# Fixed orders in the pooling stage and the convolution's tail, two-row biases, early row stores, joined closings and respread units

## The chip, the cores and the metric

The kernel runs on one core of a Trainium2 chip. The metric is the device time of one execution in microseconds (us). The kernel before takes 1178.71 us (median of three runs, 1175.62 to 1179.85). Its profiled execution took 1184.47 us, of which the span of the trace is 1182.6 us.

## The reference

A trunk of four layers on 256 tokens of width 1024, all in float32. Layers 0 and 3 mix tokens with latent attention, layer 1 with a Conformer convolution, layer 2 with a causal pooling mixer; each is followed by a feed-forward part of inner width 4096. Shift, scale and gate of every part come from a conditioning vector c.

```
c_act = silu(c)
for i in range(4):
    mod = c_act @ ada_w[i] + ada_b[i]                      # 6 rows of 1024
    sh_m, sc_m, gt_m, sh_f, sc_f, gt_f = split(mod, 6)
    h = rmsnorm(x, g[i,0]) * (1 + sc_m) + sh_m
    y = mla(h) | conv(h) | pool(h)                         # by layer
    x = x + gt_m * rmsnorm(y, g[i,1])
    h = rmsnorm(x, g[i,2]) * (1 + sc_f) + sh_f
    y = square(relu(h @ w1[i])) @ w2[i]
    x = x + gt_f * rmsnorm(y, g[i,3])

conv: u = (a[:, :D] * sigmoid(a[:, D:])),  a = h @ w_pw1 + b_pw1
      u = depthwise_causal_conv(u, w_dw, width 31) + b_dw
      y = silu(layernorm(u, ln_g, ln_b)) @ w_pw2 + b_pw2
pool: p_g = trailing mean of h over 2, 4, 8, 16 tokens (by channel group) - h
      y = (p_g @ w_g + b_g) * scale
```

## The kernel before, in words

Tokens stand as two blocks of 128, t = 0 and 1, the width as halves of 512 columns, n = 0 and 1. Every weight block of 128 x 1024 (a tile `raw`, five slots) is fetched by the sync engine (SP), rounded by ScalarE to a part `hi` (L173), and the rest `lo` is formed by VectorE (L174); six slots each. A product then takes three matmuls, hi with hi, lo with hi, hi with lo. SP's queue is written in program order. Of the other engines the order is chosen by a scheduler from its own estimates, except where `line` or `nosync` fixes one instruction behind another, and `tc.issue_after` holds a group behind an instruction.

The conditioning rows are made beside the rest of the work. A *unit* is 128 rows of `ada_w` for two of the six rows (a tile `araw`, 1 MB, NADA = 4 slots); eight units give one group of rows, tile `adap` in PSUM. In the feed-forward parts and the convolution VectorE adds units up into `acc`, two instructions of 128 x 1024 for each (L221, L223), and TensorE closes the sum with a product with ones (`ada_flush`, L265, `adap<-acc,ones_c`): a closing. Between the parts TensorE does a unit itself (`adap<-araw,c_act`). Then `ada_row` (L240 to L244) adds the bias; `spread` stores a row to DRAM and fetches it back for all 128 partitions, both on GpSimd's (POOL's) queue.

How many units are done where stands in two tables, MIX for the token mixers and FF for the feed-forward parts: units by step, units at the boundary ahead of the part, and how many are fetched ahead at its end (L702 to L725):

```
if c == CF:            # CF = 14
    ada_fetch(ahead)
...
rowblock([w2[i, 2 * cc + k] for k in range(2)], ...)
```

A feed-forward part has sixteen steps c. Step c makes h(c) = h @ w1 (L652, L655), r (L704, L705), relu and square (L706, L707), gh and gl (L709, L710), then the step's units; the product with w2 (`y`, L583 to L587) runs one step behind. So behind h(14) stands y(13), with the weights that SP fetches after the `ahead` units.

The convolution ends with a tail: taps of the depthwise product by blocks (L1060), transposes to tokens (`ctok`), LayerNorm (L1126 to L1132), transposes back (`sT_ps`, L1149), SiLU (L1155), and the product with w_pw2. The pooling stage takes its tokens from `boundary` (squares, scaling, residual, L500 to L570) block by block, forms the means as a product with a banded matrix (`pT_ps`, L1214 for the sixteen tokens that reach into block 1, the spill, and L1221), and multiplies with small weights (L1258) on top of a bias row (L1251).

Of the kernel before, what the change touches and what calls it, by code (L numbers as in the profile page):

```python
# [51 lines left out]
def tile_trunk(ctx: ExitStack, tc: tile.TileContext, x, cT, pos, invf, ada_w, ada_bg,  # L52
# [49 lines left out]
    ones_r = cp.tile([1, P], F32R, name="ones_r")  # L102
    V.tensor_copy(ones_r, ones_f[0:1])
# [134 lines left out]
    def ada_row(i, g, pt, put=lambda eng, ins: ins):  # L238
# [7 lines left out]
        rows[(i, g)] = row  # L246

# [67 lines left out]
    def spread(t, row, j):  # L315
        d = dr.tile([2, 512], F32, tag="row", name="rowd")
        ins = nc.gpsimd.dma_start(d, row[64 * j:64 * j + 64:32])
        if gate["pool"] is not None:
            nosync(ins, gate["pool"])
        nc.gpsimd.dma_start(t, d.rearrange("a n -> (a n)").unsqueeze(0).to_broadcast([P, D]))  # L320

    def bcast(tag, row, j):
        t = act.tile([P, D], F32, tag=f"bc_{tag}", name=f"bc_{tag}")
        spread(t, row, j)
# [5 lines left out]
    def gate_row(i):  # L330
        if (i, 1) in rows and i not in sent:
            sent.add(i)
            bcast("g", rows[(i, 1)], 0)


    def prep(row):
        bcast("a", row, 1)
        bct["sh"] = row
# [183 lines left out]
    def boundary(ys, units, planes=None, tokens=None, early=None, first=None):  # L522
# [16 lines left out]
        if not final:  # L539
            r = rsqrt_eps(*cols(ms))  # L540
            if tokens is not None:
                tokens(xa, r)
                low = early()
            else:
# [114 lines left out]

    def rowblock(srcs, lh, ll, y, first, last, tiles_first=False):  # L660
# [21 lines left out]
    def ffn(i, h, units, ahead, mid, first):  # L682
        hh, hl = h
        pair = both[0]
        bcast("g", rows[(i, 1)], 1)
# [100 lines left out]
    def mla(i, h, units, ahead):  # L786
# [3 lines left out]
        with tc.tile_pool(name=f"mla{i}", bufs=1) as mp:  # L790
# [239 lines left out]
            if (i, 2) in rows:  # L1030
                prep(rows[(i, 2)])
# [8 lines left out]
    def conv(i, h, units, ahead, first):  # L1040
        j = i // 3
        hh, hl = h
        with tc.tile_pool(name=f"conv{i}", bufs=1) as vp:
# [42 lines left out]
            for m in range(KT):  # L1086
                if m + 2 < KT:
                    for p in range(2):
                        fetch(w_pw1[j, m + 2, p])
                if m == 0:  # L1090
# [28 lines left out]
            prep(rows[(i, 2)])  # L1119
            shift_rows()  # L1120
            sh_, sl_ = planes()
            un = []
            for t in range(NT):
                st = sm.tile([P, 2, 6], F32, tag="st", name="st")
                for n in range(2):
                    V.bn_stats(st[:, n], ctok[t][n])  # L1126
                mv = sm.tile([P, 2], F32, tag="mv", name="mv")
                V.bn_aggr(mv, st)
                r = rsqrt_eps(mv[:, 1:2])
                xn = tmp.tile([P, D], F32, tag="xa", name="un")  # L1130
                for n in range(2):
                    V.tensor_scalar(xn[:, 512 * n:512 * n + 512], ctok[t][n], mv[:, 0:1], r,  # L1132
                                    ALU.subtract, ALU.mult)
                un.append(xn)
            ada(units[8])
            ada_flush()
            scope[0] = None
            y = y_banks()
            for t in range(NT):
                ts = slice(t * P, (t + 1) * P)  # L1140
                for n in range(2):
                    ns = slice(512 * n, 512 * n + 512)
                    T.matmul(y[t][n], ones_r, b2h[:, ns], start=True, stop=False, skip_group_check=True)
                    T.matmul(y[t][n], ones_r, b2l[:, ns], start=False, stop=False, skip_group_check=True)
                for g in range(2):
# [7 lines left out]
                    for k in range(4):  # L1153
# [7 lines left out]
                     [sl_[:, k] for k in range(4)], y, False, False, tiles_first=True)  # L1161
# [6 lines left out]
    def pool_consts(pp, j):  # L1168
# [5 lines left out]
        spread(shb, bct["sh"], 0)  # L1174
        return psc, band, shb

    def pool(i, head, consts, units, ahead):
# [15 lines left out]
        fetch(pool_b[j])  # L1193
        wp = [load(pool_w[j, k], gains) for k in range(2)]
        bias = fetched.pop((pool_b[j].tensor.name, pool_b[j].offset))
        V.tensor_tensor(bias, bias, psc[0:1, :], op=ALU.mult)
# [12 lines left out]
        def means(t, h, b=None):  # L1209
            if b is None:  # L1210
                b = bank("h", "pT_ps")
                for k in range(4 if t else 0):
                    kk = 4 * h + k
                    T.matmul(b[:, k * P:k * P + 16], hs[0][:, kk * P:(kk + 1) * P],  # L1214
                             band[:, kk // 2, 0, P:P + 16], start=(k == 0), stop=False,
                             skip_group_check=True)
                if t and len(hs) == 1:
                    return b
            for k in range(4):
                kk = 4 * h + k  # L1220
                T.matmul(b[:, k * P:(k + 1) * P], hs[t][:, kk * P:(kk + 1) * P],  # L1221
                         band[:, kk // 2, t, 0:P], start=(t == 0 and k == 0), stop=True,
                         skip_group_check=True)
            o = (slice(None), slice(4 * h, 4 * h + 4), slice(t * P, (t + 1) * P))
            b = b.rearrange("p (k t) -> p k t", k=4)
            gate["act"] = line("act", A.copy(ph[o], b))
# [4 lines left out]
            return low  # L1231

        ahead1 = []

        def early():
            low = [means(0, h) for h in range(2)]
            ahead1.append(means(1, 0))
            return low
# [5 lines left out]
        bcast("g", rows[(i, 1)], 0)  # L1244
        prep(rows[(i, 2)])
        ada(units)
        y = y_banks()
        for t in range(NT):
            ts = slice(t * P, (t + 1) * P)
            for n in range(2):  # L1250
                T.matmul(y[t][n], ones_f[0:1], bias[:, 512 * n:512 * n + 512], start=True,  # L1251
# [166 lines left out]
```

## Time and profile before

| | before |
|---|---|
| median of the runs (us) | 1178.71 |
| profiled execution (us) | 1184.47 |
| span of its trace (us) | 1182.6 |
| TensorE busy | 1138.4 us, 96% |
| VectorE busy | 850.6 us, 72% |
| ScalarE busy | 645.3 us, 55% |
| GpSimd busy | 54.1 us, 5% |

The attention of layer 0 ends at about 160 us; the feed-forward parts run from about 168 to 340, 488 to 662, 703 to 877 and 1002 to 1171 us, the convolution from 360 to 469 and the pooling stage from 662 to 692. Engine names in the rows: PE is TensorE, PEld its weight load, DVE VectorE, ACT ScalarE, POOL GpSimd, SPq the sync engine's DMA queue. A time in brackets is idle time ahead of an instruction, with what ended it.

### The profile page before, as it was taken

Reading aid. Unit: us, or ns where it says so; the run is one execution under the profiler, and the core shown is the slowest. Engines: PE = TensorE matmul, PEld = TensorE weight load, DVE = VectorE, ACT = ScalarE, POOL = GpSimd, SP = SyncE. Lnnn points to the kernel's source line nnn. Section 1 sums busy time; section 2 is a strip of 40 time slices with the busy share of each in tenths; the row PEclk is TensorE's granted clock in tenths of the full one; section 3 lists DMA queues with packets and bytes.
Section 4 is the critical chain, followed back from the end, with each engine's and each line's share of the span. In section 5 each row is a group of like instructions: output and inputs, shape, how many; then the busy total and the mean of one; then the engine's idle time right before and its main releaser. Section 6 shows DMA issues by size and latency. Waiting matters only on the chain. (4 is left out here: it accounts for less than half of the span.)

```text
span 1182.6 us, 17593 instructions
## 1 busy us (share of the span) xinstructions
PE 1138.4 (96%) x6706; PEld 923.5 (78%) x6706; DVE 850.6 (72%) x1197; ACT 645.3 (55%) x1145; POOL 54.1 (5%) x127
## 2 busy tenths in 40 slices
PE   7899999999999999999999999999997999999997
PEld 4667778788778867888887677878877878888886
DVE  3689787877766665787876778787876995755554
ACT  3355576556553244755564366555545675756553
POOL 1000010000010010000000110000011001000000
PEclk9999999999999988999999899999998999999999
DMA  9878759787617785778896479888644522766550
GB/s 332 304 290 311 298 208 347 270 329 290 245 53 236 256 322 213 272 272 351 315 343 256 187 278 364 311 311 323 246 134 157 170 81 80 250 199 191 183 193 35
DMA packets 73383, 290.00 MB, mean 245 GB/s; under 512 B 9986, under 2 KB 15234, under 8 KB 61012
## 3 DMA queue, kind: packets, MB, share of 16 engines
q1 hardware_dynamic: 70484, 280.44, 65.1%
q0 software_dynamic: 2816, 8.46, 2.0%
q8 instruction: 52, 0.85, 0.3%
q14 instruction: 31, 0.25, 0.1%
HBM read 286.57 MB, written 2.29 MB: 244 GB/s over the span
## 5 line engine op out<-in xcount | busy, mean ns | idle before, releaser
L174 DVE TENSOR_TENSOR lo<-raw,hi 128x1024 fp32r<-128x1024 f32 (+2 forms) x335 | 392.0, 1192 | 98.4 <-ACT hi L173 69.0
L173 ACT CAST hi<-raw 128x1024 fp32r<-128x1024 f32 (+2 forms) x335 | 335.1, 1028 | 78.6 <-PE y L587 39.4
L652 PE MATMUL h<-hT,hi 128*128 128x512 f32 x960 | 240.4, 392 | 0.0
L652 PEld LDWEIGHTS h<-hT,hi 128*128 128x128 f32 x960 | 175.8, 188 | 37.7 <-issue 3.4
L583 PE MATMUL y<-hi,gh 128*128 128x512 f32 x512 | 200.3, 393 | 1.5 <-ACT hi L173 1.5
L586 PE MATMUL y<-lo,gh 128*128 128x512 f32 x512 | 200.1, 391 | 0.2
L587 PE MATMUL y<-hi,gl 128*128 128x512 f32 x512 | 199.0, 390 | 0.0
L655 PEld LDWEIGHTS h<-hT,lo 128*128 128x128 f32 x960 | 131.0, 190 | 14.9 <-issue 5.9
L704 ACT COPY r<-h 128x256 f32<-128x256 f32 x120 | 44.5, 371 | 175.8 <-PE h L655 175.7
L655 PE MATMUL h<-hT,lo 128*128 128x256 f32 x960 | 136.0, 283 | 0.0
L223 DVE SCALAR_TENSOR_TENSOR acc<-araw,c_act,acc 128x1024 f32<-128x1024 f32 x106 | 130.7, 1279 | 0.4 <-DMA araw<-in_ada_w_dram 0.4
L583 PEld LDWEIGHTS y<-hi,gh 128*128 128x128 f32 x512 | 96.3, 188 | 22.8 <-ACT hi L173 2.4
L587 PEld LDWEIGHTS y<-hi,gl 128*128 128x128 f32 x512 | 96.1, 188 | 21.8 <-issue 0.8
L586 PEld LDWEIGHTS y<-lo,gh 128*128 128x128 f32 x512 | 96.4, 188 | 18.5 <-DVE lo L174 1.0
L705 DVE TENSOR_TENSOR r<-h,r 128x256 f32<-128x256 f32 x120 | 50.5, 421 | 39.8 <-ACT r L704 39.2
L710 DVE TENSOR_TENSOR gl<-r,gh 128x512 fp32r<-128x512 f32 x60 | 41.4, 690 | 50.2 <-ACT gh L709 50.2
L706 ACT ACTIVATE r<-r 128x512 f32<-128x512 f32 x60 | 37.9, 632 | 35.2 <-DVE r L705 35.2
L583 PE MATMUL y<-hi,hT 128*128 128x512 f32 x96 | 39.4, 412 | 0.0
L707 ACT ACTIVATE r<-r 128x512 f32<-128x512 f32 x60 | 37.9, 632 | 1.7
L586 PE MATMUL y<-lo,hT 128*128 128x512 f32 x96 | 38.8, 405 | 0.0
L587 PE MATMUL y<-hi,hT 128*128 128x512 f32 x96 | 38.6, 404 | 0.0
L709 ACT CAST gh<-r 128x512 fp32r<-128x512 f32 x60 | 37.2, 620 | 1.4
(257 smaller groups left out, 1486.8 us busy)
## 6 DMA issues: line engine op xcount, KB each, us to landing
raw<-in_w_dram SPq DMA_DIRECT2D x256, 512.0 KB, 5.8
araw<-in_ada_w_dram SPq DMA_DIRECT2D x96, 1024.0 KB, 6.4
raw<-in_w_pw_dram SPq DMA_DIRECT2D x24, 512.0 KB, 5.7
raw<-in_w_o_dram SPq DMA_DIRECT2D x16, 512.0 KB, 3.2
u<-ud SPq DMA_DIRECT2D x32, 132.0 KB, 2.8
raw<-in_w_ukv_dram SPq DMA_DIRECT2D x8, 512.0 KB
bc_g<-rowd POOLq DMA_DIRECT2D x8, 512.0 KB, 4.0
bc_a<-rowd POOLq DMA_DIRECT2D x7, 512.0 KB, 6.7
```

The source lines that it names most:

```text
L173: put(A.copy(h, raw), "act")
L174: put(V.tensor_tensor(l, raw, h.bitcast(F32), op=ALU.subtract), "dve")
L223: V.scalar_tensor_tensor(acc, raw[:, sl], ck, acc, op0=ALU.mult, op1=ALU.add)
L583: mm = T.matmul(o, ah, bh, start=start, stop=False, skip_group_check=True)
L586: T.matmul(o, ah, bl, start=False, stop=False, skip_group_check=True)
L587: return T.matmul(o, al, bh, start=False, stop=stop, skip_group_check=True)
L652: T.matmul(b, w(0, kk), pair[:, :, kk], start=(kk == 0), stop=False, skip_group_check=True)
L655: T.matmul(b[:, 0:S], w(1, kk), pair[:, 0, kk], start=False, stop=(kk == KT - 1), skip_group_check=True)
L704: A.copy(rf, hb[:, S:])
L705: V.tensor_tensor(rf, hb[:, 0:S], rf, op=ALU.add)
L706: A.activation(r, r, AF.Relu)
L710: gli = V.tensor_tensor(gl, g2, gh.bitcast(F32), op=ALU.subtract)
```

## The change

- Closings: the four matmuls of a closing or of a unit are issued in the order j = 2, 3, 0, 1, each fixed behind the one before, so that they stand in one run.
- Rows are stored to DRAM inside `ada_row` (`stage`, eight buffers); `spread` only fetches.
- Biases: `bias_rows` makes one tile with the rounded bias in row 0 and the rest in row 32; one fp32r matmul of 33 rows for each half and block replaces two single rows (convolution) or one float32 row (pooling).
- Convolution's tail: the first four w_pw2 blocks are fetched in the loop's last two turns, the shift rows made at turn m = 2, LayerNorm's instructions are in a fixed order, no unit and no closing remain in the tail behind LayerNorm (its closing stands ahead of the last taps), the bias comes after the first row block.
- Pooling stage: block 1's squares and scaling come ahead of block 0's copies, block 0's products between block 1's steps, all in fixed orders; constants are loaded at the start of the feed-forward part before.
- Tables: MIX and FF respread the units.

```
 def ada_mm(lhsT, raw, stop):
...
-        for j in range(4):
+        mm = None
+        for j in (2, 3, 0, 1):
+            prev = mm
             mm = T.matmul(grp["pt"][32 * j:32 * j + 32, :], lhsT, raw[j // 2][:, HALF[j % 2]],
                           start=first, stop=stop)
+            if prev is not None:
+                nosync(mm, prev)
...
+    def stage(i, g, j):
+        d = dr.tile([2, 512], F32, tag="row", name="rowd", bufs=8)
+        nc.gpsimd.dma_start(d, rows[(i, g)][64 * j:64 * j + 64:32])
+        staged[(i, g, j)] = d
...
 boundary:
         v1 = [y_scaled(1, ys, 0)]
+        if tokens is not None:
+            tokens(xa, r)
         y_squares(1, ys, 1, m1)
         r1 = rsqrt_eps(*cols(m1), eng=V)
         v1.append(y_scaled(1, ys, 1))
+        if tokens is not None:
+            low = early()
...
         residual(1, v1, r1)
+        if tokens is not None:
+            low[0][0]()
         ms = squares(1)
         r = rsqrt_eps(*cols(ms))
         if tokens is not None:
+            low[1][0]()
+            early()
             xa = scaled(1)
-            low[0]()
+            low[0][1]()
             tokens(xa, r)
-            low[1]()
+            low[1][1]()
...
+    def bias_rows(src, gain=None):
+        raw = raws.tile([P, D], F32, tag="raw", name="bias")[0:33]
+        G.memset(raw, 0.0)
+        for p in (0, 32):
+            nc.sync.dma_start(raw[p:p + 1], src)
+        if gain is not None:
+            V.tensor_tensor(raw, raw, gain[0:33], op=ALU.mult)
+        r = raws.tile([P, D], F32R, tag="raw", name="bias_r")[0:33]
+        A.copy(r, raw)
+        V.tensor_tensor(r[32:33], raw[32:33], r[32:33].bitcast(F32), op=ALU.subtract)
+        return r
...
 conv:
+                else:
+                    for k in range(2):
+                        fetch(w_pw2[j, 2 * (m + 2 - KT) + k])
+                if m == 2:
+                    prep(i, 2)
+                    shift_rows()
...
-            b2h, b2l = load(b_pw2[j])
             wp = [load(w_pw2[j, k]) for k in range(4)]
+            bias = bias_rows(b_pw2[j])
+            ada_flush()
...
-            ada(units[8])
-            ada_flush()
...
             rowblock(wp, [sh_[:, k] for k in range(4)],
-                     [sl_[:, k] for k in range(4)], y, False, False, tiles_first=True)
+                     [sl_[:, k] for k in range(4)], y, True, False, tiles_first=True)
+            for t in range(NT):
+                for n in range(2):
+                    T.matmul(y[t][n], ones_r, bias[:, 512 * n:512 * n + 512], start=False,
+                             stop=False, skip_group_check=True)
             ada_fetch(ahead)
...
 pool:
+        def early():
+            if not spilt:
+                parts = [means(0, h) for h in range(2)]
+                spilt.append(spill(0))
+                return parts
+            y.extend(y_banks())
+            biased(0)
+            product(0, 0)
 
         head(tokens=tokens, early=early)
-        for low in [means(1, 0, ahead1[0]), means(1, 1)]:
+        for k in range(2):
+            fetch(w1[i, 0, k])
+        ada_fetch(ahead)
+        spilt.append(spill(1))
+        parts = [means(1, h, spilt[h]) for h in range(2)]
+        for high, _ in parts:
+            high()
+        for _, low in parts:
             low()
...
+        biased(1)
+        product(0, 1)
+        product(1, 0)
+        product(1, 1)
         ada(units)
-        y = y_banks()
...
     MIX = {
         0: ([2, 4, 2, 3, 3, 2], 0, 1),
-        1: ([0, 0, 2, 0, 1, 2, 1, 0, 1], 2, 3),
-        2: (2, 4, 3),
+        1: ([0, 0, 2, 1, 1, 1, 1, 0, 0], 1, 3),
+        2: (1, 4, 2),
...
     FF = {
-        0: ([1, 1, 1, 1, 1, 2, 1, 1, 1, 1, 1, 1, 1, 1, 0, 0], 1, 3),
-        1: ([1, 1, 1, 2, 1, 1, 2, 1, 1, 2, 1, 1, 1, 1, 0, 0], 2, 4),
-        2: ([1, 1, 1, 1, 2, 1, 2, 1, 2, 1, 1, 2, 1, 2, 1, 0], 2, 0),
+        0: ([1, 2, 1, 1, 2, 1, 1, 2, 1, 1, 2, 1, 1, 2, 1, 0], 1, 3),
+        1: ([2, 1, 1, 2, 1, 1, 2, 1, 1, 1, 1, 1, 1, 1, 1, 0], 2, 4),
+        2: ([1, 1, 1, 1, 1, 1, 1, 1, 1, 1, 2, 1, 1, 2, 2, 0], 1, 0),
```

SP's queue at the end of the second feed-forward part (layer 1), before: `raw<-in_w_dram` are weights of w1 and w2, `araw` units.

```order
138 L197 DMA araw<-in_ada_w_dram 128x2048
139 L1170 DMA psc<-in_pool_s_dram 128x1024
140 L1172 DMA band<-in_pool_band_dram 128x1152
141 L155 DMA raw<-in_w_dram 128x1024 x4
142 L197 DMA araw<-in_ada_w_dram 128x2048
143 L155 DMA raw<-in_w_dram 128x1024 x4
144 L197 DMA araw<-in_ada_w_dram 128x2048 x2
145 L200 DMA bg<-in_ada_bg_dram 4x1024
146 L197 DMA araw<-in_ada_w_dram 128x2048 x2
147 L155 DMA raw<-in_w_dram 128x1024 x8
```

The same queue and place after the change.

```order
145 L200 DMA bg<-in_ada_bg_dram 4x1024
146 L155 DMA raw<-in_w_dram 128x1024 x4
147 L197 DMA araw<-in_ada_w_dram 128x2048
148 L155 DMA raw<-in_w_dram 128x1024 x4
149 L197 DMA araw<-in_ada_w_dram 128x2048 x5
150 L155 DMA raw<-in_w_dram 128x1024 x8
```

Ahead of the eight weights stand five `araw` now, the unit of c = 14 and the four fetched ahead, where there were the four; with four slots the last of the five takes the slot of the first.

VectorE at the same place, before: `r` and `gl` are the feed-forward part's, `acc` a unit, `lo` a weight.

```order
469 L710 TENSOR_TENSOR gl<-r,gh 128x512
470 L223 SCALAR_TENSOR_TENSOR acc<-araw,c_act,acc 128x1024 x2
471 L705 TENSOR_TENSOR r<-h_6137,r 128x256
472 L705 TENSOR_TENSOR r<-h_6156,r 128x256
473 L174 TENSOR_TENSOR lo<-raw,hi 128x1024 x2
474 L710 TENSOR_TENSOR gl<-r,gh 128x512
475 L174 TENSOR_TENSOR lo<-raw,hi 128x1024 x5
```

VectorE there after the change.

```order
464 L742 TENSOR_TENSOR gl<-r,gh 128x512
465 L223 SCALAR_TENSOR_TENSOR acc<-araw,c_act,acc 128x1024 x2
466 L737 TENSOR_TENSOR r<-h_6155,r 128x256
467 L737 TENSOR_TENSOR r<-h_6174,r 128x256
468 L742 TENSOR_TENSOR gl<-r,gh 128x512
469 L223 SCALAR_TENSOR_TENSOR acc<-araw,c_act,acc 128x1024 x2
470 L240 TENSOR_TENSOR row_6206<-adap,bg 128x512
471 L242 TENSOR_TENSOR row_6206<-row_6206,bg 128x512
472 L174 TENSOR_TENSOR lo<-raw,hi 128x1024 x8
```

The eight `lo` moved from both sides of gl(14) (rows 473 to 475) to behind the unit of c = 14 (row 469).

ScalarE in the pooling stage, before: `junk` are squares summed up (`y` the stage's input by halves, `xs` the tokens), `hT<-pT_ps` the means.

```order
387 L135 ACTIVATE junk,msy<-y_4861 128x512
388 L135 ACTIVATE junk,msy<-y_4862 128x512
389 L135 ACTIVATE junk,ms<-xs 128x512 x2
390 L135 ACTIVATE junk,msy<-y_4863 128x512
391 L1226 CAST hT<-pT_ps 128x4x128 x2
392 L135 ACTIVATE junk,msy<-y_4864 128x512
393 L135 ACTIVATE junk,ms<-xs 128x512 x2
394 L1226 CAST hT<-pT_ps 128x4x128 x2
```

ScalarE there after the change.

```order
379 L135 ACTIVATE junk,msy<-y_4898 128x512
380 L135 ACTIVATE junk,msy<-y_4899 128x512
381 L135 ACTIVATE junk,ms<-xs 128x512 x2
382 L135 ACTIVATE junk,msy<-y_4900 128x512
383 L135 ACTIVATE junk,msy<-y_4901 128x512
384 L1262 CAST hT<-pT_ps 128x4x128
385 L135 ACTIVATE junk,ms<-xs 128x512 x2
386 L1262 CAST hT<-pT_ps 128x4x128 x3
```

The second half's squares of block 1 (row 392 before, 383 now) moved ahead of the copies of block 0's means.

## Rows read from the trace of the kernel before

**Rows 1.** Busy time by stretch: us; PE, PEld, DVE, ACT, POOL; clock; DMA; GB/s.

```profile
436.70:450.40 13.70, 13.70 (x42) 8.69 (x35) 7.54 (x14) 7.06 (x18) 1.17 (x2) 0.50 0.86 348
...
672.20:682.50 10.30, 10.30 (x36) 7.53 (x35) 4.96 (x9) 0.96 (x3) 3.22 (x6) 0.50 0.67 277
703.00:880.00 177.00, 175.98 (x885) 144.49 (x884) 143.92 (x159) 101.62 (x148) 1.63 (x4) 1.00 0.79 293
890.70:894.10 3.40, 3.40 (x15) 2.83 (x15) 2.14 (x7) 2.59 (x9) 1.52 (x3) 0.50 0.17 46
```

**Rows 2.** TensorE's timeline, end of the second feed-forward part: start, us, instruction.

```profile
635.97 1.11 PE L655 MATMUL h<-hT,lo 128*128 128x256 f32 x8
637.01 1.07 PE L265 MATMUL adap<-acc,ones_c 128*32 128x512 f32 x8
639.60 1.19 PE L583 MATMUL y<-hi,gh 128*128 128x512 f32 x4 [1.52 <-ACT hi L173]
```

**Rows 3.** The sync engine's queue there: start, us, issues.

```profile
623.21 9.17 SPq L197 DMA_DIRECT2D araw<-in_ada_w_dram  x2
632.48 12.87 SPq L155 DMA_DIRECT2D raw<-in_w_dram  x8
```

**Rows 4.** VectorE's timeline there.

```profile
629.55 2.48 DVE L223 SCALAR_TENSOR_TENSOR acc<-araw,c_act,acc 128x1024 f32<-128x1024 f32 x2
...
639.58 1.23 DVE L174 TENSOR_TENSOR lo<-raw,hi 128x1024 fp32r<-128x1024 f32 x1 [1.63 <-ACT hi L173]
...
643.18 0.68 DVE L710 TENSOR_TENSOR gl<-r,gh 128x512 fp32r<-128x512 f32 x1
```

**Rows 5.** TensorE's timeline, one half of a split closing.

```profile
221.02 1.05 PE L265 MATMUL adap<-acc,ones_c 128*32 128x512 f32 x4
```

**Rows 6.** Tile adap, closings: what ended TensorE's wait, us, times.

```profile
  DVE acc L223: 1.7, 2
```

**Rows 7.** TensorE's timeline, units ahead of the convolution.

```profile
340.43 1.92 PE L265 MATMUL adap<-araw,c_act 128*32 128x512 f32 x16
```

**Rows 8.** TensorE's timeline, taps; the later two with a closing between.

```profile
396.46 3.69 PE L1060 MATMUL dw_ps<-u,dg 128*32 128x256 f32 x64
...
416.18 2.79 PE L1060 MATMUL dw_ps<-u,dg 128*32 128x256 f32 x42
...
420.73 1.36 PE L1060 MATMUL dw_ps<-u,dg 128*32 128x256 f32 x10
```

**Rows 9.** ScalarE's timeline, convolution's tail.

```profile
445.92 2.91 ACT L1155 ACTIVATE sv<-sT_ps,cv_lb,cv_lg 128x128 f32<-128x128 f32 x8 [4.59 <-PE sT_ps L1149]
```

**Rows 10.** TensorE's timeline, first work behind the convolution's last product.

```profile
468.87 1.92 PE L265 MATMUL adap<-araw,c_act 128*32 128x512 f32 x16
```

**Rows 11.** ScalarE's timeline, pooling stage.

```profile
663.39 0.60 ACT L135 ACTIVATE junk<-y 128x512 bf16<-128x512 f32 x1
...
668.64 0.60 ACT L135 ACTIVATE junk<-y 128x512 bf16<-128x512 f32 x1
```

**Rows 12.** VectorE's timeline, pooling stage.

```profile
673.71 1.42 DVE L1203 SCALAR_TENSOR_TENSOR xa<-xa,r,shb 128x512 f32<-128x512 f32 x2 [0.24 <-POOL r L121]
```

**Rows 13.** TensorE's timeline, pooling stage.

```profile
673.32 3.78 PE L1251 MATMUL y<-raw,ones_f 1*128 1x512 f32 x4
677.03 1.89 PE L1214 MATMUL pT_ps<-band,xa 128*128 128x16 f32 x8
...
679.55 3.35 PE L1221 MATMUL pT_ps<-band,xa 128*128 128x128 f32 x16
...
691.88 1.16 PE L395 MATMUL hT_ps<-dg,xa 128*128 128x128 f32 x8 [1.20 <-ACT dg L389]
```

**Rows 14.** ScalarE's timeline, step 14 of the second feed-forward part.

```profile
637.12 0.37 ACT L704 COPY r<-h 128x256 f32<-128x256 f32 x1 [2.42 <-PE h L655]
637.99 0.63 ACT L706 ACTIVATE r<-r 128x512 f32<-128x512 f32 x1 [0.49 <-DVE r L705]
```

**Rows 15.** TensorE's timeline, ahead of the last attention.

```profile
890.55 2.17 PE L412 MATMUL hT_ps<-ident,xa 128*128 128x128 f32 x8 [3.62 <-DVE xa L406]
```

More of the change, by code (lines that the diff above doesn't have):

```diff
@@ L246, in ada_row @@
         rows[(i, g)] = row
+        for j in ((0, 1) if g == 1 else (1,)):
+            stage(i, g, j)
+        if (i, g) == (2, 0):
+            stage(i, g, 0)
     def sum_tiles():
@@ L332, in gate_row, with prep @@
             sent.add(i)
[L333 to L338, printed above, removed]
+            bcast("g", i, 1, 0)
+    def prep(i, g):
+        bcast("a", i, g, 1)
+        bct["sh"] = rows[(i, g)]
     def shift_rows(row=None):
@@ L1140, in conv @@
                 ts = slice(t * P, (t + 1) * P)
[L1141 to L1144, printed above, removed]
                 for g in range(2):
@@ L1192, in pool @@
             fetch(pool_w[j, k])
-        fetch(pool_b[j])
         wp = [load(pool_w[j, k], gains) for k in range(2)]
-        bias = fetched.pop((pool_b[j].tensor.name, pool_b[j].offset))
-        V.tensor_tensor(bias, bias, psc[0:1, :], op=ALU.mult)
+        bias = bias_rows(pool_b[j], psc)
         hs = []
@@ L1230, in low, with product @@
                                                           op=ALU.subtract))
-            return low
-        ahead1 = []
-        def early():
-            low = [means(0, h) for h in range(2)]
-            ahead1.append(means(1, 0))
-            return low
-        head(tokens=tokens, early=early)
-        for low in [means(1, 0, ahead1[0]), means(1, 1)]:
+            return high, low
+        def product(t, low):
+            ts = slice(t * P, (t + 1) * P)
+            for g in range(4):
+                for k in range(2):
+                    ws = slice((2 * (g % 2) + k) * 256, (2 * (g % 2) + k) * 256 + 256)
+                    for q in ((0, 1), (0,))[low]:
+                        line("pe", T.matmul(y[t][g // 2][:, 256 * (g % 2):256 * (g % 2) + 256],
+                                            (ph, pl)[low][:, 2 * g + k, ts], wp[g // 2][q][:, ws],
+                                            start=False, stop=(low == 1 and k == 1),
+                                            skip_group_check=True))
@@ new lines, in biased @@
+        def biased(t):
+            for n in range(2):
+                line("pe", T.matmul(y[t][n], ones_r, bias[:, 512 * n:512 * n + 512],
+                                    start=True, stop=False, skip_group_check=True))
+        y = []
+        spilt = []
+        def early():
+            if not spilt:
[5 more added lines that the diff above has]
+            product(0, 0)
@@ L1242, in pool @@
+        head(tokens=tokens, early=early)
+        for k in range(2):
+            fetch(w1[i, 0, k])
[5 more added lines that the diff above has]
+        for _, low in parts:
             low()
         gate["free"] = 0
-        bcast("g", rows[(i, 1)], 0)
-        prep(rows[(i, 2)])
-        ada(units)
-        y = y_banks()
[L1248 to L1251, printed above, removed]
-                         stop=False, skip_group_check=True)
-            for low in range(2):
-                for g in range(4):
-                    for k in range(2):
-                        ws = slice((2 * (g % 2) + k) * 256, (2 * (g % 2) + k) * 256 + 256)
-                        for q in ((0, 1), (0,))[low]:
-                            T.matmul(y[t][g // 2][:, 256 * (g % 2):256 * (g % 2) + 256],
-                                     (ph, pl)[low][:, 2 * g + k, ts], wp[g // 2][q][:, ws],
-                                     start=False, stop=(low == 1 and k == 1),
-                                     skip_group_check=True)
```

74 lines of the change are left out of this document (36 added, 38 removed).

## The prediction

> **What bounds the kernel now.** I read the table by stage first, then TensorE's timeline at the places the diff touches, then the queues that feed it. In a feed-forward stage TensorE is the bound: in the third one it works 175.98 of 177 us at full clock, with twenty units summed on VectorE beside it [rows 1]. So a matmul taken out there is worth its duration, and a VectorE or DMA instruction is worth nothing until it makes TensorE wait. Between the stages latency decides, and two stretches run at half clock, 13.7 us in the convolution's tail and 10.3 us in the pooling stage [rows 1]; the reader is to see 0.50 in the column after POOL. The wait that matters most for this change is small now: at 639.60 the last but one row block of the second feed-forward stage waits 1.52 us for the hi of its weights [rows 2]. On the sync engine's queue, which issues in program order, the last fetch ahead is held until 632 and the eight weights only follow at 632.48 [rows 3]. It is held by its slot: VectorE's sum for c = 13 ends at 632.03 [rows 4].
>
> All durations are from the profiled execution (1184.47 us, span 1182.6); the median of the runs is 1178.71. I add the sum to the median, since it is a difference.
>
> **The change, part by part.**
>
> *Closings (TensorE).* A closing split by j is two runs of 1.05 us with other matmuls between (one of them in [rows 5]); whole it is one run of 1.07 [rows 2]: 1.03 less. The feed-forward stages hold seven split closings and one whole one, 7 x 2.10 + 1.07 = 15.8; afterwards nine whole ones (respreading makes one more), 9 x 1.07 = 9.6: -6.1. VectorE's sums held closings up twice, 1.7 us in all [rows 6]; I take -1.0 (0 to -1.7). The first layer's last closing becomes whole, -1.0. At the entry of the convolution one unit remains of two, half of 1.92 [rows 7]: -0.96. In the convolution a closing stood among the taps, in 5.91 us (416.18 to 422.09) that otherwise take 3.69 [rows 8], so 2.2; afterwards there is a split one, 2.1, and a whole one, 1.07: +0.95. Together **-8.1**, and with the waits at either end -7 to -9.
>
> *Convolution tail.* One unit on TensorE, four bias matmuls and the shift rows leave it, and the normalisation of the second token block is pinned behind the first, so its transposes come earlier. On the other side, all sixteen SiLU activations now stand ahead of hi and lo of the last weights, on ScalarE and VectorE: in the trace the last eight of them end at 448.8 [rows 9]. With the clock at full throughout I get the last y product 4.5 us before 468.87 [rows 10]; if it still drops, about nothing. I take **-3.5**, bounds -6 to +1. Memset, two small DMAs, copy and subtraction of the two-row bias lie on POOL, the sync queue, ScalarE and VectorE ahead of the first row block, beside its taps; without that cover one ScalarE pass and one VectorE pass, about 2.4 us at the length of a lo, 1.23 [rows 4], and the +1 holds part of that.
>
> *Pooling stage.* Of token block 1, the squares of the first half end at about 664.1, the second half's only start at 668.64, behind the two copies of block 0 [rows 11]. The change puts them first: 4.5 us. Block 1's band matmuls start at 679.55 although their input is ready at 673.71 + 1.42 = 675.1 [rows 12]: four bias matmuls, 3.78 us, and a spill of 1.89 at half clock stand in front [rows 13]. These biases become four fp32r matmuls and block 0's products fill the wait. So input at 675.1 - 4.5 = 670.6, 1.8 us for the spill and hand-over, start at 672.4. From there to the first transposes of the feed-forward stage it took 12.3 us (691.88); I keep 11.3, since two of the four units in between go, and half of their 1.92 us lies on the chain: 683.7 instead of 691.88, -8.2. TensorE now waits about 2.7 us ahead of 672.4, and I charge 0.8 for a lower clock behind it: **-7.4**. Least gain -2 (the shorter matmuls alone), most -9.5 (half clock gone too).
>
> *Earlier row stores.* The store goes to POOL's queue as soon as a row is known, the broadcast later: the broadcast starts sooner by one store. The trace shows no broadcast that ends a wait in the rows above; nothing, and a store at a bad place in POOL's order at most 1 us.
>
> *Units respread: what I expect to cost.* After the change the second feed-forward stage has a unit at c = 14, where there was none, and the same four fetches ahead. The fourth takes the slot of that unit, so on the sync queue the eight weights now stand behind VectorE's sum for c = 14, and that stands behind gl(14). h(14) ends at 637.08 [rows 2]; ScalarE's r is at 637.12 (0.37), relu at 637.99 (0.63) [rows 14]; square and gh are of the same shape, 0.63 each, gl is 0.68 and the sum 2.48 [rows 4]. 637.99 + 3 x 0.63 + 0.68 + 2.48 = 643.0, with a hand-over 643.1. Before, the slot was free at 632.03. All that follows, weights, hi, y, is late by the same 11.1 us: **+11.1**, and y starts at about 650.7 in the old count. On TensorE nothing can fill this: behind h(14) stand one closing and y. Lower end 9 (if less traffic makes the weights land sooner), upper 13.
>
> In the first feed-forward stage three are fetched ahead, so the third waits for the second unit of c = 13, which ends about 2.4 us later than a single one. But VectorE's order puts all eight lo behind gl(14) and the sum of c = 14: the first is ready at 643.1 + 1.23 [rows 4] = 644.3, in the second stage's times. Without a wait TensorE would need it two matmuls after the closing, at 638.1 + 0.4 = 638.5: **+5.9** (3 to 8). In the third stage nothing is fetched ahead, and I see no such wait.
>
> *The clock behind these waits.* After a wait of 3.62 us TensorE resumed at 890.55 [rows 15] and ran at half clock until 894.1, that is 3.4 us at 0.50 [rows 1], which costs 1.7. Two new waits of this size or more: **+3.4**, 0 to 13.7 (if each is followed by as long a stretch as the tail's 13.7 us, 6.85 each).
>
> The Trainium skill (TensorE: Matmul & The Clock Gate, HAM oscillation) ties the half clock to waits in which TensorE has no work. At 890.7 the trace agrees. In the pooling stage and the tail it does not: there the clock fell with TensorE busy 10.30 of 10.30 and 13.70 of 13.70 us [rows 1]. By the rule alone both stretches would have been at full clock before, and the change could win nothing there from the clock and would lose 0.8 in the pool's new wait. By the rows the half clock is there and may go or stay; I let the bounds of the two stages carry it.
>
> Sum: -8.1 - 3.5 - 7.4 + 11.1 + 5.9 + 3.4 = **+1.4 us**, so 1178.7 + 1.4 = 1180.1.
>
> **Rivals.**
>
> *The waits are not there.* For: the same queue held now costs 1.52 us only. Against: two fixed orders, slot and VectorE's row order, make it. Then -8.1 - 3.5 - 7.4 = -19.0: 1159.7. If only the first stage's falls away (lo made earlier than the order's estimate), -5.9 - 1.7: 1172.5.
>
> *The clock does not come back.* After each new wait TensorE stays at half clock as long as in the tail, 13.7 us instead of 3.4: 2 x (6.85 - 1.7) = +10.3, 1190.4, slower. For: the tail and the pool show such long stretches. Against: behind 890.55 it came back in 3.4 us, and dense h and y matmuls follow here as there. It decides from about 7.9 us of half clock behind each wait: 2 x (7.9 - 3.4)/2 = 4.5, with 1.4 that is 5.9.
>
> *Pool and tail win nothing.* Both keep their half clock and the new order only moves the wait: +1.4 + 10.9 = +12.3, 1191.0. For: in both stages the clock fell with no long wait before, so a shorter chain need not raise it. Against: four matmuls of 3.78 us are gone whatever the clock.
>
> **How the numbers follow.** 0.5% is 5.9 us, about what a measurement of this kernel tells from no change. Both waits and most of the gains (the forecast, 1173 to 1186 by itself): 0.45. No wait at all 0.12, one wait 0.15, low clock behind the waits 0.13, pool and tail without gain 0.15. Of the forecast 0.05 lies under 1172.8 or over 1184.6, 0.03 and 0.02. One wait alone ends on the border, most of it counted as faster: faster 0.12 + 0.15 + 0.03 = 0.30, slower 0.13 + 0.15 + 0.02 = 0.30, within 0.40. The range 1166 to 1191 leaves out the case without waits and the far end of the slower ones.
>
> **What would show it.** In the second feed-forward stage's end TensorE should wait some 12 us in front of y (released by hi) and in the first's about 6 (released by lo), with a sync-queue row for the fetches ahead that ends with VectorE's sum of c = 14, and a clock below 1.00 in the slice behind. Closings should be x8 runs of 1.07. In the pool, squares of block 1 directly behind one another on ScalarE and the gap from the last y product to the first transposes some 21 us instead of 29. Wrong would be: no wait in front of y(13), or half clock over 8 us behind it, or a tail whose end does not move.

## The result and the profile after

| | before | after |
|---|---|---|
| median of the runs (us) | 1178.71 | 1190.37 |
| lowest to highest (us) | 1175.62 to 1179.85 | 1187.09 to 1191.30 |
| ratio to before, 95% interval | | 1.0098 [1.0075, 1.0120] |
| profiled execution (us), span, granted clock | 1184.47, 1182.6, 0.983 | 1190.91, 1189.1, 0.975 |

The change makes the kernel 11.7 us slower by the medians. The forecast was +1.4, the range 1166 to 1191: the result lies 10.3 us above the forecast and 0.6 us inside the upper end of a wide range. Both new waits are where the prediction put them.

TensorE at the end of the second feed-forward part, after [rows 2]: start, us, instruction, and in brackets the idle time ahead of it.

```profile
637.03 1.11 PE L674 MATMUL h<-hT,lo 128*128 128x256 f32 x8
644.15 1.94 PE L271 MATMUL adap<-acc,ones_c 128*32 128x512 f32 x8 [6.01 <-DVE acc L223]
652.24 1.22 PE L602 MATMUL y<-hi,gh 128*128 128x512 f32 x2 [6.15 <-ACT hi L173]
```

The sync engine's queue there, after [rows 3], VectorE [rows 4], and ScalarE.

```profile
644.12 0.33 SPq L197 DMA_DIRECT2D araw<-in_ada_w_dram  x1
644.54 11.80 SPq L155 DMA_DIRECT2D raw<-in_w_dram  x8
```

```profile
641.01 0.69 DVE L742 TENSOR_TENSOR gl<-r,gh 128x512 fp32r<-128x512 f32 x1 [2.00 <-ACT gh L741]
641.62 2.47 DVE L223 SCALAR_TENSOR_TENSOR acc<-araw,c_act,acc 128x1024 f32<-128x1024 f32 x2
...
652.22 1.23 DVE L174 TENSOR_TENSOR lo<-raw,hi 128x1024 fp32r<-128x1024 f32 x1 [4.65 <-ACT hi L173]
```

```profile
651.14 1.04 ACT L173 CAST hi<-raw 128x1024 fp32r<-128x1024 f32 x1 [10.16 <-DMA raw<-in_w_dram]
```

The sum for c = 14 ends at 641.62 + 2.47 = 644.09, the last fetch ahead is issued at 644.12, and the weights follow at 644.54: the slot holds the queue. ScalarE then waits 10.16 us for the first of these weights, and its hi ends TensorE's wait. h(14) ends at 638.14, so y starts 14.1 us behind it, where it was 2.5 before. One link had no price in the prediction: the respread also makes the second part's last closing wait 6.01 us for that sum, ahead of y on TensorE. It lies inside the time in which y would wait anyway.

The first feed-forward part, after: TensorE, then VectorE, then the sync engine's queue.

```profile
313.95 1.11 PE L674 MATMUL h<-hT,lo 128*128 128x256 f32 x8
319.67 1.65 PE L602 MATMUL y<-hi,gh 128*128 128x512 f32 x3 [4.61 <-ACT hi L173]
322.20 0.80 PE L605 MATMUL y<-lo,gh 128*128 128x512 f32 x1 [0.88 <-DVE lo L174]
```

```profile
307.53 4.87 DVE L223 SCALAR_TENSOR_TENSOR acc<-araw,c_act,acc 128x1024 f32<-128x1024 f32 x4
...
318.54 2.47 DVE L223 SCALAR_TENSOR_TENSOR acc<-araw,c_act,acc 128x1024 f32<-128x1024 f32 x2
320.93 5.76 DVE L174 TENSOR_TENSOR lo<-raw,hi 128x1024 fp32r<-128x1024 f32 x5
```

```profile
310.03 2.72 SPq L197 DMA_DIRECT2D araw<-in_ada_w_dram  x2
312.85 11.93 SPq L155 DMA_DIRECT2D raw<-in_w_dram  x8
```

The waits are 4.61 + 0.88 = 5.5 us, and the first lo indeed starts only where the sum of c = 14 ends. But the larger wait is ended by hi, not by lo: here too the weights follow a fetch ahead that is held, by the two units of c = 13, whose sums end at 307.53 + 4.87 = 312.40. The prediction saw that fetch and charged only the lo; the two links end within 3 us of each other, and the lo is the last. The stretches at half clock, after [rows 1] (the column after POOL is the granted clock):

```profile
317.40:327.70 10.30, 7.14 (x17) 5.18 (x18) 9.50 (x9) 6.78 (x7) 0.00 (x0) 0.52 0.96 341
447.10:450.50 3.40, 3.40 (x11) 2.87 (x12) 3.14 (x8) 3.40 (x9) 0.00 (x0) 0.56 0.16 63
641.70:658.70 17.00, 8.36 (x23) 4.81 (x24) 9.75 (x10) 5.91 (x6) 1.06 (x2) 0.51 0.79 277
699.70:706.50 6.80, 6.22 (x26) 5.56 (x27) 3.57 (x7) 2.91 (x8) 0.64 (x2) 0.53 0.03 11
```

Half clock came during each new wait and stayed behind it, for 327.70 - 319.67 = 8.0 us in the first part and 658.70 - 652.24 = 6.5 in the second; the first is at the border of the 8 us that the prediction named as a sign of being wrong. TensorE worked 7.14 and 8.36 us in the two stretches; half of that, 3.6 and 4.2, is an estimate of what the clock costs. In the tail it lasted 3.4 us instead of 13.7, in the pooling stage 6.8 instead of 10.3, but behind a longer wait, ahead of 700.28.

The pooling stage after: TensorE [rows 13], ScalarE [rows 11] and VectorE.

```profile
687.24 2.03 PE L1254 MATMUL pT_ps<-band,xa 128*128 128x128 f32 x16
...
700.28 2.08 PE L409 MATMUL hT_ps<-dg,xa 128*128 128x128 f32 x8 [4.06 <-ACT dg L403]
```

```profile
678.53 0.60 ACT L135 ACTIVATE junk<-y 128x512 bf16<-128x512 f32 x1
...
679.25 0.60 ACT L135 ACTIVATE junk<-y 128x512 bf16<-128x512 f32 x1
```

```profile
694.79 1.29 DVE L528 TENSOR_TENSOR v<-y,bc_g 128x512 f32<-128x512 f32 x2 [1.56 <-DMA bc_g<-rowd]
```

The squares of block 1 stand directly behind one another now (they began 5.2 us apart). The band matmuls of block 1 start 9.8 us behind the start of the stage's units (677.40), where it was 17.0: 7.2 us sooner, as forecast, and without the wait of 2.7 us that I had ahead of them. But the chain ends later than I had it: from there to the first transposes it takes 13.0 us (687.24 to 700.28), where I kept 11.3. VectorE waits for the broadcast of the gate row, and TensorE waits 4.06 us ahead of the transposes, where it was 1.20 [rows 13].

**Stages.** The trunk taken apart at two kinds of marks on TensorE's timeline, us. "FF" is a feed-forward part, from the first transposes `hT_ps<-dg,xa` ahead of it (691.88 in [rows 13]) to the end of its last y product. The convolution runs from the first part's last y product to its own, the pooling stage from the second part's last y product to the first transposes of the third part. The versions are those of the experiments below. Half clock behind a wait ahead of the transposes counts in the part that follows.

| stage | before | before, again | after | no unit at 14 | joined alone | gate early |
|---|---|---|---|---|---|---|
| FF 1 | 189.1 | 189.1 | 195.9 | 188.6 | 186.5 | 188.5 |
| convolution | 128.4 | 128.7 | 125.0 | 125.2 | 122.2 | 125.1 |
| FF 2 | 191.4 | 192.6 | 203.0 | 188.9 | 189.4 | 188.8 |
| pooling | 29.3 | 27.6 | 22.8 | 22.9 | 28.2 | 21.5 |
| FF 3 | 191.8 | 191.7 | 190.1 | 190.5 | 190.6 | 188.7 |

### The profile page after: what moved, and what is told of

Read it like the earlier page. It is cut to its first block, busy times and chain, and to the rows that moved or that the text cites. A ratio compares the mean times of both kernels' runs of the same rounds, so it can differ in the third digit from the quotient of the medians.

```text
span 1189.1 us, 17600 instructions
## 1 busy us (share of the span) xinstructions
PE 1124.7 (95%) x6682; PEld 921.7 (78%) x6682; DVE 859.0 (72%) x1206; ACT 647.5 (54%) x1146; POOL 56.1 (5%) x129
## 4 chain that ended last, share of the span: by engine, by line
PE 82%; DVE 6%; ACT 4%; DMA 3%; issue 2%; POOL 2%; SPq 0%; POOLq 0%; DVEq 0%; ACTq 0%
PE h L671 18%; PE y L602 11%; PE y L605 11%; PE y L606 11%; PE h L674 9%; PE adap L271 2%; PE dw_ps L1092 2%; ACT junk L135 2%; PE s_ps L1004 2%; DMA raw<-in_w_dram 1%; DVE acc L223 1%; PE h L645 1%; PE pw L619 1%; PE pw L621 1%; PE pw L625 1%
## 5 line engine op out<-in xcount | busy, mean ns | idle before, releaser
L174 DVE TENSOR_TENSOR lo<-raw,hi 128x1024 fp32r<-128x1024 f32 (+1 forms) x334 | 391.2, 1193 | 101.2 <-ACT hi L173 67.6
L173 ACT CAST hi<-raw 128x1024 fp32r<-128x1024 f32 (+1 forms) x334 | 335.4, 1029 | 108.0 <-PE y L606 48.2
L223 DVE SCALAR_TENSOR_TENSOR acc<-araw,c_act,acc 128x1024 f32<-128x1024 f32 x110 | 135.7, 1279 | 0.8 <-DMA araw<-in_ada_w_dram 0.8
L602 PE MATMUL y<-hi,hT 128*128 128x512 f32 x96 | 38.8, 404 | 0.0
L528 DVE TENSOR_TENSOR v<-y,bc_g 128x512 f32<-128x512 f32 x32 | 22.0, 689 | 22.1 <-ACT junk L135 20.3
```

Of the source, the lines that this page charges most:

```text
L173: put(A.copy(h, raw), "act")
L174: put(V.tensor_tensor(l, raw, h.bitcast(F32), op=ALU.subtract), "dve")
L223: V.scalar_tensor_tensor(acc, raw[:, sl], ck, acc, op0=ALU.mult, op1=ALU.add)
L602: mm = T.matmul(o, ah, bh, start=start, stop=False, skip_group_check=True)
```

## Experiments

Each was timed against the kernel before on the same chip in five rounds, except the fourth, one more profile of the kernel before. Ratios are to the kernel before, with their 95% interval.

**1. No unit at c = 14** (on the changed kernel).

```
-0: ([1, 2, 1, 1, 2, 1, 1, 2, 1, 1, 2, 1, 1, 2, 1, 0], 1, 3),
-1: ([2, 1, 1, 2, 1, 1, 2, 1, 1, 1, 1, 1, 1, 1, 1, 0], 2, 4),
+0: ([2, 2, 1, 1, 2, 1, 2, 2, 1, 1, 2, 1, 1, 1, 0, 0], 1, 3),
+1: ([2, 1, 1, 2, 1, 1, 2, 1, 1, 2, 1, 1, 1, 1, 0, 0], 2, 4),
```

> The changed kernel with the unit of c = 14 moved to an earlier step in the first and the second feed-forward part (totals, closings and everything else as in the change). Theory (the fetches ahead are held by the slot of that unit): the waits of 5.5 us in the first part and 12.2 us in the second fall to at most 2 us together, the half clock behind them (about 7 us of loss) goes with them, and the kernel takes 1166 to 1172 us, faster than the kernel before by 0.6 to 1.1%. Rival A (the respread units as such load VectorE too much, wherever they stand): the waits only move to other steps and the time stays above 1183. Rival B (waits go, but the pooling stage and the tail won nothing in timed runs): about 1178, the time of the kernel before.

Measured: 1171.78 us, ratio 0.9925 [0.9895, 0.9955]. The wait in the first part is gone, in the second 1.41 us stay, as before. Moving two units in the first part (the one of c = 14 and the second of c = 13) and one in the second turns a loss of 11.7 us into a gain of about 9. Rival A falls. In the first part the edit takes away both links at once, the held fetch and the late lo, so it doesn't tell which of the two cost the wait there. From here on this version is called version 1.

**2. A unit at c = 14 in the kernel before.**

```
-1: ([1, 1, 1, 2, 1, 1, 2, 1, 1, 2, 1, 1, 1, 1, 0, 0], 2, 4),
+1: ([1, 1, 1, 2, 1, 1, 2, 1, 1, 2, 1, 1, 1, 0, 1, 0], 2, 4),
```

> The kernel before with one edit: in the second feed-forward part one unit moves from c = 13 to c = 14, nothing else. Theory (slot of the last unit holds the four fetches ahead, and with them the eight weights behind): TensorE's wait ahead of y(13) grows from 1.5 to about 12 us and half clock behind it costs 3 to 5 us more: 1190 to 1195 us. Rival (the wait in the changed kernel comes from the number of units or from the joined closings): no change, 1176 to 1181 us.

Measured: 1194.07 us, ratio 1.0115 [1.0087, 1.0144]. Its sync-engine queue and TensorE:

```profile
621.50 20.16 SPq L197 DMA_DIRECT2D araw<-in_ada_w_dram  x2
641.75 12.52 SPq L155 DMA_DIRECT2D raw<-in_w_dram  x8
```

```profile
640.16 3.12 PE L265 MATMUL adap<-acc,ones_c 128*32 128x512 f32 x8 [4.81 <-DVE acc L223]
650.25 1.22 PE L583 MATMUL y<-hi,gh 128*128 128x512 f32 x2 [6.98 <-ACT hi L173]
```

The fetch that held for 9.17 us [rows 3] holds for 20.16. The same unit, one step later, is enough; neither more units nor joined closings are needed for the wait.

**3. Three fetched ahead instead of four, unit at c = 14 left** (on the changed kernel).

```
-1: ([2, 1, 1, 2, 1, 1, 2, 1, 1, 1, 1, 1, 1, 1, 1, 0], 2, 4),
+1: ([2, 1, 1, 2, 1, 1, 2, 1, 1, 1, 1, 1, 1, 1, 1, 0], 2, 3),
```

> The changed kernel with three instead of four units fetched ahead at the end of the second feed-forward part; the unit of c = 14 stays. Theory (the slot): the third fetch takes the slot of c = 13, the weights are asked for some 10 us sooner, and the wait of 12.2 us ahead of y(13) falls to 3 us or less; the kernel takes 1173 to 1179 us. Rival (VectorE is too late with the sum of c = 14 and its lo behind it, whatever the queue does): 6 us or more of the wait stay, 1183 to 1187 us.

Measured: 1179.26 us, ratio 0.9998 [0.9982, 1.0014]; a hair over the range expected, well off the rival's. The second part's wait, with the unit still at c = 14:

```profile
643.86 1.20 PE L602 MATMUL y<-hi,gh 128*128 128x512 f32 x4 [2.52 <-ACT hi L173]
```

The wait follows the fetches ahead, as the slot wants it. The rival is not shut out by this run alone: the scheduler also put two of the eight lo ahead of gl(14) and the sum of c = 14 here, and the closing into h(15). What speaks for the slot in the changed kernel is that hi ended the wait, and hi waited 10.16 us for its weights, not for VectorE.

**4. The kernel before, a second profile.**

> The kernel before unchanged, for a second profile. Theory that the half clock in the convolution's tail (13.7 us) and in the pooling stage (10.3 us) is there in every execution: both appear again, each within 3.5 us. Rival (they come and go from one execution to the next, so that part of the gain read from the two profiles is no gain in the timed runs): one of them is missing or shorter by half, and the span is some 3 to 6 us shorter.

Measured: 1182.25 us in its one execution. The tail's 13.7 us at half clock came again, the pooling stage's were two stretches of 3.4 instead of one of 10.3. So the theory held for the tail and not for the pool. A stretch of 3.4 us was new, at 641.10, behind the second part's wait of 1.52 us; in the first profile the clock stayed up there behind the same wait. The next run shows that the tail's is not in every execution of the old code either.

**5. Joined closings alone** (on the kernel before).

```
-        for j in range(4):
+        mm = None
+        for j in (2, 3, 0, 1):
+            prev = mm
...
+            if prev is not None:
+                nosync(mm, prev)
```

> The kernel before with the closings' and units' four matmuls in the order j = 2, 3, 0, 1, each behind the one before, and nothing else. Theory of the prediction (a split closing occupies TensorE for 2.10 us, a whole one for 1.07, and TensorE is the bound there): seven closings in the feed-forward parts and two elsewhere save 1.0 each, 7 to 9 us less: 1170 to 1172. Rival (a split closing's halves only look long because their ends are modelled, or other waits take the time back): 3 us or less, 1176 to 1179.

Measured: 1170.05 us, ratio 0.9909 [0.9880, 0.9938]. Between their first and last products with w2 the three feed-forward parts take 169.8, 172.6 and 171.7 us instead of 172.4, 174.7 and 175.0: 8.0 us less for the seven split closings, 1.14 each, where the rows said 1.03. In the profile the convolution is 6.2 us shorter too; but for its closing and unit, joined as well, its code is that of before, and its tail ran at full clock this time. The tail of this version, then that of the first profile before:

```profile
415.00:461.70 46.70, 43.31 (x473) 31.42 (x469) 32.01 (x41) 24.34 (x49) 6.46 (x12) 1.00 0.91 331
```

```profile
423.00:468.90 45.90, 44.20 (x403) 33.17 (x403) 27.14 (x36) 22.12 (x45) 6.04 (x12) 0.85 0.81 312
```

**6. The old pooling stage in version 1** (functions `boundary` and `pool`, bias included, replaced by those of before).

```
-        bias = bias_rows(pool_b[j], psc)
+        bias = fetched.pop((pool_b[j].tensor.name, pool_b[j].offset))
+        V.tensor_tensor(bias, bias, psc[0:1, :], op=ALU.mult)
...
```

> The changed kernel with the unit of c = 14 moved (as in the first experiment, 1171.8) and with the boundary, the pooling stage and its bias of the kernel before. Theory from the two profiles (the new pooling stage saves 6 us but half clock follows its new wait and takes about 3 back): 2 to 5 us slower than the first experiment, 1174 to 1177. The prediction's figure was 7.4: 1179. Rival (nothing gained, the old half clock of 10 us does not come in every execution): 1171 to 1173.

Measured: 1172.76 us, ratio 0.9940 [0.9917, 0.9963] against 0.9925 [0.9895, 0.9955] for version 1: not told apart by time, and in the rival's range. The old stage ran at full clock in this profile and took 25.0 us against 22.9; behind both came 6.8 us at half clock. So on equal terms the new order is worth some 2 us in the profile.

**7. The old convolution in version 1** (function `conv` replaced).

```
-            bias = bias_rows(b_pw2[j])
-            ada_flush()
+            b2h, b2l = load(b_pw2[j])
...
```

> The same first experiment (1171.8) with the convolution's code of the kernel before (loop, tail and its bias rows; the table stays). Prediction: the new tail is worth 3.5 us less 0.95 for the closings there, so 2 to 3 us slower than the first experiment, 1174 to 1175. Rival (the half clock of 13.7 us that made the old tail slow in the first profile depends on the work ahead of it, and without it both tails are alike): 1170 to 1173.

Measured: 1176.63 us, ratio 0.9962 [0.9940, 0.9984], by the ratios some 4 us slower than version 1, over the range expected, though the two intervals touch. The half clock was there again, and the convolution took 131.6 us:

```profile
440.50:454.20 13.70, 13.15 (x35) 9.02 (x35) 8.06 (x15) 7.24 (x17) 1.16 (x2) 0.50 0.47 190
```

**8. The gate row's broadcast early** (on version 1).

```
             low[1][0]()
             early()
+            gate["pool"] = None
+            gate_row(grow)
```

> The first experiment (1171.8) with one fetch moved: the gate row's broadcast of the pooling stage is issued on GpSimd's queue ahead of the last rsqrt of the stage, not behind it, some 3 us sooner. Theory (in the first experiment VectorE waits 1.3 us for that broadcast in the chain that ends with the feed-forward part's first transposes): the wait goes and TensorE's wait of 3.4 us ahead of those transposes falls to about 2.1; 0.5 to 1.3 us less, 1170 to 1171.5, hardly to be told from no change by time, but by the wait. Rival (the next link, the sums of squares, is as late): TensorE's wait stays within 0.3 us of 3.4.

Measured: 1166.85 us, ratio 0.9888 [0.9859, 0.9917], the lowest median of all versions. By the medians it gains 4.9 us on version 1, more than the 1.3 that I expected, but the intervals of the two ratios overlap. GpSimd, VectorE and TensorE of this version:

```profile
659.55 0.63 POOL L331 DMA_DIRECT2D bc_g<-rowd  x1 [0.27 <-DVE v L528]
```

```profile
670.12 1.28 DVE L528 TENSOR_TENSOR v<-y,bc_g 128x512 f32<-128x512 f32 x2
```

```profile
675.22 1.05 PE L409 MATMUL hT_ps<-dg,xa 128*128 128x128 f32 x7 [2.04 <-ACT dg L403]
```

The wait for the DMA is gone, TensorE's wait is 2.04 us, as expected, and the half clock behind it is 3.4 us instead of 6.8. The stage takes 21.5 us instead of 22.9, and the third feed-forward part 188.7 instead of 190.5: 3.2 us in the two profiles, of which 1.4 are the wait.

**9. A version put together** from the shortest stages.

```
 MIX 1: ([0, 0, 2, 0, 1, 2, 1, 0, 1], 2, 3), MIX 2: (1, 4, 2)
 FF 0, 1: as before; FF 2: ([1, 1, 1, 1, 2, 1, 2, 1, 2, 1, 1, 2, 1, 2, 2, 0], 2, 0)
 conv: as before; the rest as in 8
```

> A version put together from the stages that were shortest so far: the kernel before with its convolution and its tables for the convolution and the first two feed-forward parts (no unit at c = 14), joined closings, the new pooling stage with the gate row's broadcast early, rows stored early, 21 units in the third feed-forward part. By the stages of the traces (first feed-forward part 187 against 189, convolution 122 to 124 against 125, pooling 19 to 20, the rest as in the version with the early gate row, 1166.9): 1160 to 1164. Rival (the old tail falls to half clock for 13.7 us, as it did in three of five executions with it): 1166 to 1170.

Measured: 1171.59 us, ratio 0.9929 [0.9902, 0.9957]: worse than 8, and for another reason than the rival's alone. The tail did fall to half clock (128.2 us), and the pooling stage took 28.3 (the 19 to 20 that I had expected count to an earlier instruction; by the table it was 21.5 to 23):

```profile
669.41 1.09 POOL L327 DMA_DIRECT2D rowd<-row  x2 [3.11 <-DVE row L242]
674.53 0.55 POOL L331 DMA_DIRECT2D bc_g<-rowd  x1 [4.03 <-DMA rowd<-row]
```

```profile
679.92 1.29 DVE L528 TENSOR_TENSOR v<-y,bc_g 128x512 f32<-128x512 f32 x2 [6.72 <-DMA bc_g<-rowd]
```

With the old tables four units fewer are done by then, the gate row is known only inside the stage, and its store and broadcast end the chain. The new pooling stage needs the respread units; I had taken the two for separate.

**10. The same with the new convolution.**

```
 MIX 1: ([0, 0, 2, 0, 1, 2, 1, 1, 0], 2, 3); conv: as in the change
```

> The same version with the change's convolution and tail in place of the old one, one unit moved from the convolution's tail into its loop. Theory (the new tail is 1 to 3 us longer than the old one at full clock and saves 3 to 6 us only where the old one falls to half clock): if the old tail stays at full clock in the run beside it, this is 1 to 3 us slower than it; if it falls, 3 to 6 us faster. The prediction said 3.5 us faster, whatever the clock.

Measured: 1178.64 us, ratio 0.9986 [0.9964, 1.0008], 7 us slower than 9 by the medians although 9's old tail was at half clock in its profile. By the two profiles the convolution took 127.7 against 128.2, no difference; its profiled execution (1173.2) lies 5 us under the median. The granted clock of its executions went from 0.974 to 0.986, and the profiled one had 0.986; where the others lost their clock is not seen, so this run settles nothing about the tail.

**11. Unused matmuls in the two waits** (on the changed kernel).

```
+                    if c == CF and i in FILL:          # FILL = {0: 5, 1: 11}
+                        fb = bank("h", "fill")
+                        for _ in range(FILL[i]):
+                            mm = T.matmul(fb, ident, xs[:, 0, 0:512], start=True, stop=True, ...)
```

> The changed kernel with matmuls whose result is never used put into TensorE's two new waits, 5 of 128 x 512 float32 in the first feed-forward part and 11 in the second, behind h(14) and ahead of y(13). Nothing else changes; the weights come as late as before. Theory (half clock behind the waits costs some 7 us by the rows, 3.3 and 4.0): the half clock there goes and the kernel takes 1182 to 1185 instead of 1190.4. Rival (the half clock costs little, since the weights' DMAs would hold TensorE as long at full clock): 1188 to 1191.

Measured: 1188.37 us, ratio 1.0070 [1.0058, 1.0082]. The clock stayed up:

```profile
317.50:329.90 12.40, 11.34 (x43) 6.45 (x43) 9.19 (x9) 8.44 (x10) 0.00 (x0) 1.00 0.93 355
638.00:657.40 19.40, 16.73 (x57) 8.57 (x55) 10.72 (x11) 8.30 (x10) 1.06 (x2) 1.00 0.64 243
```

The first part took 193.7 instead of 195.9 us and the second 199.6 instead of 203.0: 5.6 less by the stages, 2 to 3 by the times, which lie in the rival's range (in the first part the scheduler also put a closing, 1.06 us, in between y's matmuls). So the half clock behind the waits costs 2 to 6 us, between my theory and its rival.

## Why the prediction held in part

*The two waits and their clock.* Right in place and, together, in size; the cause is shown for the second part. Forecast 11.1 + 5.9 + 3.4 = 20.4 us; the changed kernel is 18.6 slower than version 1 by the medians, 20.4 by the two ratios (1.73% of 1179), and 7.3 + 14.1 = 21.4 by the two stages. The parts were shifted: 15.4 us of new wait (5.5 + 12.2, less 0.7 and 1.5 that were there) instead of 17.0, and 2 to 6 us of clock by the filled waits (7.8 by the rows) instead of 3.4. I took the 3.4 us at half clock that follow a wait of 3.62 [rows 15]; with the longer waits it took 7.1 and 8.4 us of work.

*Closings.* Right: 1.14 each against 1.03, alone worth 10 us by the times with what the convolution's clock gave.

*The step that failed is the size of the other gains.* I had -19.0 us without the waits (the first rival); version 1 measures -0.75% of 1179, -8.8, and -12.1 between the two profiled executions. The joined closings alone measure 0.9909, version 1 with everything else on top 0.9925: by the times nothing shows of the pooling stage, the tail and the respread together.

- The pooling stage: from the last y product to the transposes I forecast -8.2, and the profiles give 29.3 - 22.8 = -6.5; against the old stage at full clock it is about -2 (25.0 to 22.9). The chain did start 7.2 us sooner, but its last part took 13.0 us instead of the 11.3 that I kept: it waited for a broadcast that nothing had waited for before, VectorE 1.56 us, TensorE 4.06. I had read that no broadcast ended a wait in the rows of before, and charged nothing; moved earlier, the stage overtook it. Half clock follows, 6.22 us of work in 6.8, some 3 us by an estimate, where I had charged 0.8. Experiment 8 gives back 3.2 us in its profile.
- The tail: -3.5 forecast and -3.4 between the profiles, but with the clock, not by the order alone. With the old code the convolution took 122.2 and 124.3 us (experiments 5 and 2) where the clock stayed up, 128.2 to 131.6 where it fell; the new code takes 123.5 to 127.7. The units in the loop differ between these versions, so a microsecond more or less is open; a gain on equal terms is not there. In four of six profiles the old tail fell to half clock for 13.7 us, and in none of seven did the new one fall for so long at a stretch; whether the new order does that is not shown, and the times of experiments 7 and 10 contradict each other on it.
- The respread in the first part: I charged the one more closing, 1.07, and nothing for five more units. With 20 units instead of 15 that part takes 188.6 us, with the old table and joined closings 186.5 (experiment 5): 2.1 us, of which the closing is 1.1. In version 1 TensorE also waits twice for hi there, 1.0 us in all, against 0.5 for a sum with the old table; the rest I did not trace.

*Profile against median.* I set the sum, made from a profiled execution with two long stretches at half clock, against the median without a correction. That execution took 1184.47 us, 5.8 above the median; of the 57 executions timed beside the experiments four took longer. Its mean granted clock was 0.983; in the 17 executions timed beside the first experiments it was 0.985 to 0.988 in 12. A mean of 0.983 is some 40 us at half clock, 0.987 some 31; by this estimate the 9 us between them cost at most 4.6. So gains that consist of half clock taken away were in part no gains in the runs that count. This can be why the profiles differ by only 6.4 us and the medians by 11.7; no run shows it directly.

*Luck.* The forecast missed by 10.3 us, and the range, 25 us wide, held the result with 0.6 to spare. By its number the result is that of two rivals. The second (1190.4, half clock for 13.7 us behind each wait) is not what happened: 8.0 and 6.5 us. The third (1191.0, pool and tail win nothing) is close to it by the times: the pool's half clock moved behind a new wait, as that rival says, though the stage itself became shorter. I gave it 0.15.

## What to carry to other kernels

Before a unit of side work is moved one step later, follow the buffer slot that it holds: whoever fetches into that slot holds everything behind it on an in-order queue, here eight weight blocks. A gain that rests on a stretch at half clock is to be taken from two or more profiles, since the stretch can differ between two executions of the same kernel (experiment 4) and between versions that share its code (experiment 5), and the sum is then set against an execution of the same kind. And when a chain is shortened, look up the DMAs that arrived just in time for the old one.

## What the runs showed of the hardware

The old tail, with nearly the same instructions, ran at half clock for 13.7 us in two profiles of the kernel before (TensorE busy for all of it) and at full clock in experiments 5 and 2, where TensorE was idle more (43.31 us of work in 46.70 and 41.61 in 45.80, against 44.20 in 45.90). Busy time alone did not keep the clock. The Trainium skill (TensorE: Matmul & The Clock Gate, HAM oscillation) explains a fall by waits in which TensorE has no work; the two waits here and experiment 11 agree with it (0.52 and 0.51 without the filling, 1.00 with it). The old tail does not, where no wait in the 13.7 us ahead of the fall was over 0.63 us, nor does the old pooling stage, where TensorE was busy for all of the 6.1 us ahead of it; what made the clock fall there stays open.
